# A three-part encoder layer in split fp32: pinning the loads of the SwiGLU tiles and beginning the weight sums one slab earlier

## The chip, the cores and the metric

The kernel runs on one core of one Trainium2 chip. The metric is the device time of one execution in microseconds (us), the median of several runs; lower is better. Beside it there is one execution recorded by the hardware profiler, with a trace of every instruction on every engine. TensorE multiplies, VectorE (DVE) and ScalarE (ACT) work elementwise, GpSimd (POOL) does here little more than issue DMAs, and SyncE (SP) issues the other DMAs.

## The reference

One encoder layer over 256 tokens of width 2048 in float32, ending with a norm. Cut to what matters here:

```
x = x + mix(rms_norm(x)) @ w_out                 # four mixers side by side
x = x + cross_attention(rms_norm(x), mem_n)
h = rms_norm(x)
gate, up = split(h @ w_gate_up)                  # 2048 -> 2 * 5632
x = x + (silu(gate) * up) @ w_down               # 5632 -> 2048
out = rms_norm(x)
```

The change lies in the third part, the SwiGLU.

## The kernel before

**Weights.** All weights lie in one tensor, in the order of use. It is cut into slabs of 128 x 2048 floats (1024 KB), and a slab holds sixteen 128 x 128 blocks. A slab is read into a `raw` buffer by SP (four such buffers during this stage) and each float is split into a high part `wh` (ACT, a cast) and a low part `wl` (DVE, a subtraction), because TensorE multiplies in a shorter format; three products (high by high, high by low, low by high: lines 472 to 474) stand for one fp32 product. The pieces that ACT and DVE produce are called halves here. The kernel makes them five ahead of TensorE (`_fill`, with a ring of five buffers), so that ACT and DVE wait for TensorE when all is well.

**The SwiGLU's first half, `gate_up`.** The 5632 columns are worked in groups of 512, eight slabs to a group: group 0 apart, and then groups j = 1 to 10, each through `paired_rows` after a plan of eight letters:

```
GROUPS = *["NSSNSSNN"] * 9, "NSNSNSNN"
```

A slab marked N is used as it is, by 24 products. A slab marked S holds two rows and two columns of blocks that are worked as in Strassen's method, with 21 products instead of 24; `z` holds the combined forms of the activations, and sums of the weights are needed too. So a group of four N and four S has 4 x 24 + 4 x 21 = 180 products. The S slabs of a group are called S1, S2, S4 and S5 below, by their place in the plan.

**The sums of an S slab.** Two of the sums are not made by DVE but by a DMA that adds. While some earlier slab is loaded (`_load`), SP reads the slab's last 512 columns into a buffer `t` (line 114; one of four tiles named `res`), ACT copies them to the buffer's other half (line 119), and GpSimd issues a DMA that adds 1024 further columns of the slab onto them (line 121, `accum_op=ALU.add`). This last one is called the adding DMA below. The ACT copy stands in a kept place: `keep` (which is `keep_place`) ties an instruction to the one that stands before it on its engine, so that the scheduler of the compiler, which otherwise reorders the instructions of an engine as they come ready, leaves it there. `AHEAD` says how many slabs before its own slab this is begun: two. So the sums of S1, S2, S4 and S5 are begun at the slabs 7 (of the group before), 0, 2 and 3 of a group, and a slab counts as loaded in program order right before its first half is made. ACT splits the summed buffer in the third of the S slab's four steps (line 178, `wh<-res`), and DVE adds with it in the second (line 189, `raw<-res,raw`).

**The way of a SwiGLU tile.** At the end of a group, `up` makes silu(gate) * up, turns it (DVE, line 597) and GpSimd stores it (line 599, two DMAs named `hidden<-g`), four tiles of 128 x 256 in a group and 44 in all. For the second half of the SwiGLU the tiles are read back (`load_turned`, line 604, `tmp<-hidden`) into `tmp` buffers, of which there are eleven, and split into `f` tiles. The first 22 are read and split during `gate_up` by the generator `fetch`, which `begin` calls at the first three N slabs of a group; the other 22 are queued after the loop with a second `fetch`. GpSimd issues its DMAs one after the other, and one that waits for something holds up all that stand behind it in GpSimd's line.

`self.bg.now` is TensorE's time as the kernel counts it while the program is written (0.68 us for three products), and `stored[j]` is its value when group j's storing was written down.

Of the kernel before, what the change touches and what calls it, by code (L numbers as in the profile page):

```python
# [28 lines left out]
FT = DFF // P  # L29
# [19 lines left out]

PAIRED = {a + i for a, plan in [(GATE_UP + 8 * j, GROUPS[j % len(GROUPS)]) for j in range(10)] + [(DOWN, PASSES[0]), (DOWN + 22, PASSES[1])]  # L50
          for i, x in enumerate(plan) if x in "Ss"}
AHEAD = (-2, -2)

SUMS = [{GATE_UP + 8 * j + i + a: GATE_UP + 8 * j + i for j in range(10) for i, x in enumerate(GROUPS[j % len(GROUPS)]) if x == "S"}
        for a in AHEAD]

# [236 lines left out]
class Block:  # L293
# [805 lines left out]
    def gate_up(self, gp, f, z):  # L1099

        nc = self.nc
        box, g, stored = {}, {}, []

        def gate(ps):
            for r in range(2):
                g[r] = gp.tile([P, 512], F32, name=f"g{r}", tag=f"g{r}")
                nc.scalar.activation(g[r], ps[r], AF.Silu, scale=box["col"][:, r:r + 1])

        def up(j, ps, h=None):
            h = h or [gp.tile([P, 512], F32, name="h", tag="h", bufs=2) for _ in range(2)]  # L1110
            for r in range(2):
                self.stt(h[r], ps[r], box["col"][:, r:r + 1], g[r], ALU.mult, ALU.mult)
                self.store_turned(self.ff, 4 * j, r, g[r], h[r])
            stored.append(self.bg.now)

        def mixed(q1, q5, q6, q7):

            g[0], g[1], h[0], h[1] = (gp.tile([P, 512], F32, name=n, tag=n, bufs=b) for n, b in (("g0", 1), ("g1", 1), ("h", 2), ("h", 2)))
            nc.scalar.copy(g[0], q1)
            self.tt(h[0], g[0], q6, ALU.add)  # L1120
            self.tt(g[1], h[0], q7, ALU.add)
            self.tt(h[0], q5, h[0], ALU.subtract)
            self.tt(h[1], q5, g[1], ALU.subtract)

        def gated(*ps):

            for r in range(2):
                self.tt(g[r], g[r], ps[r], ALU.add)
                nc.scalar.activation(g[r], g[r], AF.Silu, scale=box["col"][:, r:r + 1])

        def upped(j, ps):

            for r in range(2):
                self.tt(h[r], h[r], ps[r], ALU.add)
            up(j, h, h)

        h = {}

        def fetch(k0, k1, ahead, pause, wait=0):

            m = {}
            for k in range(k0, k1 + ahead):
                if k < k1:
                    while len(stored) <= k // 4:
                        yield
                    m[k] = self.tmp()
                    self.load_turned(m[k], self.ff, k)
                if k >= k0 + ahead:
                    while k0 == 0 and k - ahead >= 20 and "free" not in box:
                        yield  # L1150
                    while wait and self.bg.now < stored[(k - ahead) // 4] + wait:
                        yield
                    mark = self.mark()
                    self.split(f[k - ahead], m.pop(k - ahead))
                    self.keep_place(mark)
                    self.have = k - ahead + 1
                    yield pause

        def norm():

            mark = self.mark()
            nc.scalar.activation(self.mg[:, 0:1], self.mg[:, 0:1], AF.Silu)
            self.keep_place(mark)
            yield 2.0
            self.row_norm(1, box)
            yield

        arp = ExitStack()
        ar = arp.enter_context(self.tc.tile_pool(name="arp", bufs=4))
        arrival = lambda: ar.tile([P, R], F32, name="ar", tag="ar")  # L1170
        last = self.bg.add(self.arrive(self.xf[1], 3, arrival, self.put3, FAR), go=True)
        col = self.bg.add(norm())

        def combined():
            for ks, z in sums:
                yield 3.0
                yield from self.combine(z, *(self.h3[k] for k in ks))

        sums = [((2 * i, 2 * i + 1), z[(i + 1) % 4]) for i in range(4)]
        comb = self.bg.add(combined())  # L1180
        whole = [self.whole(c) for c in range(4)]

        def before(n):
            if n == 1:
                self.st.lend(self.wz)
                self.st.sums = list(whole)
            if n in (1, 3):
                self.bg.drain(self.late if n == 1 else last)
            if n == 3:
                self.leave(3)  # L1190

        ps = self.gemm_rows("w_gate_up", [0, DFF], self.h3,
                            parts=[(range(8), [0]), (range(8, 12), [0]), (range(12), [1]), (range(12, 16), [0]), (range(12, 16), [1])],
                            before=before)
        self.bg.drain(col)
        arp.close()
        more = ExitStack()
        rx = more.enter_context(self.tc.tile_pool(name="rawx", bufs=1))
        self.st.raws.append([rx, -1])
        gate(ps[0])  # L1200
        up(0, ps[1])
        early = fetch(0, FT - 22, 3, 2.0, 15)
        self.bg.drain(comb)
        for j in range(1, DFF // 512):
            plan = GROUPS[(j - 1) % len(GROUPS)]
            if j == 10:
                box["free"] = True
            turns = [i for i, x in enumerate(plan) if x == "N"][:3]

            def begin(i):  # L1210

                if (j, i) == (10, 5):
                    self.st.back(self.wz, rx)
                if i in turns:
                    next(early, None)

            upped(j, self.paired_rows("w_gate_up", [j * 512, DFF + j * 512], self.h3, sums[:8 - plan.count("N")], plan, mixed, gated,
                                      before=begin, swap=j % 2 == 0)[0])
        more.close()
        for c, x in enumerate(whole):  # L1220
            nc.sync.dma_start(x, self.rd[:, c * 1024:(c + 1) * 1024])
        for _ in early:
            pass
        self.fetch = self.bg.add(fetch(FT - 22, FT, 6, SOON))

    def down(self, f, sp):
# [752 lines left out]
```

## Time and profile before

| | us |
|---|---|
| median of 3 runs (1444.95 to 1450.44) | 1446.47 |
| profiled execution | 1453.54 |
| its span in the trace | 1451.7 |
| TensorE products, busy | 1427.3 |
| VectorE busy | 1176.1 |
| ScalarE busy | 850.3 |
| GpSimd busy | 243.3 |

The profiled execution is 1.84 us longer than its span and 7.07 us longer than the median of the runs. In rows of a timeline the columns are: start, duration, engine, line, operation, what is written from what, how many, and in brackets the engine's idle time before it with what ended that time. `PEclk` in a row of stages is the TensorE clock that was granted, as a share of full speed.

### The profile page before, as it was taken

The page shows a single profiled execution, that of the slowest core. Times are in us where ns is not written, and L with a number is a line of the kernel's source. Part 1 is how long each engine was busy: PE and PEld are TensorE (multiplying, and loading weights), DVE is VectorE, ACT ScalarE, POOL GpSimd, SP SyncE. Part 2 cuts the span into 40 slices and gives each one's busy share as a digit, 9 for nine tenths or more (in the row PEclk, how much of TensorE's full clock was granted, in tenths as well). Part 3 has the DMA queues.
Part 4 walks back from the last instruction along what each step waited for, and adds up shares of the span by engine and source line. Part 5 has one row for each costly group of instructions (what it writes and reads, how often), then busy time and mean ns, then how long its engine had stood idle before and what let it go on. Part 6 is the DMA issues. An engine that isn't in the chain of part 4 may idle for free.

```text
span 1451.7 us, 18644 instructions
## 1 busy us (share of the span) xinstructions
PE 1427.3 (98%) x6562; PEld 1178.6 (81%) x6562; DVE 1176.1 (81%) x1782; ACT 850.3 (59%) x1242; POOL 243.3 (17%) x315
## 2 busy tenths in 40 slices
PE   9999999999999999999999999999999999999997
PEld 7888888888888888888888877778878888788885
DVE  6668868777977676676688988889988988989997
ACT  6556555446655555555565666656656654655655
POOL 0000100012302233530422211222211111100000
PEclk9999999999999999999999999999999999999999
DMA  9887564456657788964998999999999986665554
GB/s 345 293 287 249 201 216 152 168 187 225 200 196 226 243 266 260 271 195 149 292 298 250 273 272 272 262 273 240 272 258 280 275 269 205 200 237 191 187 223 145
DMA packets 72461, 344.84 MB, mean 238 GB/s; under 512 B 10893, under 2 KB 12590, under 8 KB 45744
## 3 DMA queue, kind: packets, MB, share of 16 engines
q1 hardware_dynamic: 52976, 285.31, 57.0%
q0 software_dynamic: 18960, 57.69, 17.3%
q8 instruction: 51, 0.84, 0.2%
q10 hardware_dynamic: 432, 0.66, 0.1%
q14 instruction: 42, 0.34, 0.1%
HBM read 321.07 MB, written 22.54 MB: 237 GB/s over the span
## 4 chain that ended last, share of the span: by engine, by line
PE 75%; issue 13%; DMA 5%; DVE 3%; POOL 2%; ACT 1%; SPq 0%; POOLq 0%; ACTq 0%; DVEq 0%
PE pg L473 18%; PE pg L472 18%; PE pg L474 18%; PE pg L420 4%; PE pm L472 4%; PE pm L473 4%; PE pm L474 4%; PE pg L421 2%; DMA res<-in_W 2%; DMA hidden<-g 1%; DVE wl L179 1%; DMA raw<-in_W 1%; PE pm L1432 1%; POOL tmp L604 1%; POOL res L121 1%
## 5 line engine op out<-in xcount | busy, mean ns | idle before, releaser
L167 DVE TENSOR_TENSOR wl<-raw,wh 128x1024 fp32r<-128x1024 f32 (+1 forms) x395 | 474.5, 1212 | 165.1 <-ACT wh L166 163.2
L166 ACT CAST wh<-raw 128x1024 fp32r<-128x1024 f32 (+1 forms) x395 | 406.2, 1042 | 260.0 <-PE pg L474 193.0
L472 PE MATMUL pg<-wh,act 128*128 128x512 f32 (+1 forms) x1165 | 456.1, 392 | 2.1 <-ACT wh L166 1.9
L473 PE MATMUL pg<-wl,act 128*128 128x512 f32 (+1 forms) x1165 | 454.3, 390 | 1.5 <-DVE wl L167 1.5
L474 PE MATMUL pg<-wh,act 128*128 128x512 f32 (+1 forms) x1165 | 453.9, 390 | 0.0
L472 PEld LDWEIGHTS pg<-wh,act 128*128 128x128 f32 x1165 | 219.1, 188 | 50.6 <-ACT wh L166 3.4
L473 PEld LDWEIGHTS pg<-wl,act 128*128 128x128 f32 x1165 | 219.3, 188 | 47.8 <-DVE wl L167 3.0
L474 PEld LDWEIGHTS pg<-wh,act 128*128 128x128 f32 x1165 | 219.0, 188 | 46.3 <-DVE act L322 0.2
L178 ACT CAST wh<-raw 128x1024 fp32r<-128x1024 f32 (+1 forms) x177 | 161.6, 918 | 144.7 <-DVE raw L189 58.9
L179 DVE TENSOR_TENSOR wl<-raw,wh 128x1024 fp32r<-128x1024 f32 (+1 forms) x177 | 182.9, 1057 | 23.5 <-ACT wh L178 21.8
L473 PE MATMUL pm<-wl,act 128*128 128x512 f32 x290 | 113.0, 390 | 0.2 <-DVE wl L167 0.2
L474 PE MATMUL pm<-wh,act 128*128 128x512 f32 x290 | 112.9, 389 | 0.0
L472 PE MATMUL pm<-wh,act 128*128 128x512 f32 x290 | 112.9, 389 | 0.0
L420 PE MATMUL pg<-act,wh 128*128 128x512 f32 x256 | 90.5, 395 | 0.0
L121 POOL DMA_DIRECT2D res<-in_W x39 | 35.6, 913 | 252.6 <-ACT res L119 244.2
L421 PE MATMUL pg<-act,wl 128*128 128x256 f32 x256 | 71.8, 280 | 0.0
L178 ACT CAST wh<-res 128x1024 fp32r<-128x1024 f32 x39 | 41.1, 1053 | 49.6 <-DMA res<-in_W 33.8
L189 DVE TENSOR_TENSOR raw<-raw 128x512 f32<-128x512 f32 x99 | 68.1, 688 | 1.7
L473 PEld LDWEIGHTS pm<-wl,act 128*128 128x128 f32 x290 | 54.4, 188 | 11.9 <-DVE wl L167 0.5
L472 PEld LDWEIGHTS pm<-wh,act 128*128 128x128 f32 x290 | 54.4, 188 | 11.3
L474 PEld LDWEIGHTS pm<-wh,act 128*128 128x128 f32 x290 | 54.4, 188 | 11.3
L420 PEld LDWEIGHTS pg<-act,wh 128*128 128x128 f32 x256 | 48.1, 188 | 10.5
(376 smaller groups left out, 1937.1 us busy)
## 6 DMA issues: line engine op xcount, KB each, us to landing
raw<-in_W SPq DMA_DIRECT2D x207, 1024.0 KB, 5.3
raw<-in_W SPq DMA_DIRECT2D x39, 768.0 KB, 7.2
res<-in_W POOLq DMA_DIRECT2D x39, 512.0 KB, 9.7
res<-in_W SPq DMA_DIRECT2D x39, 256.0 KB, 5.3
raw<-in_W SPq DMA_DIRECT2D x11, 512.0 KB, 7.4
hidden<-g POOLq DMA_DIRECT2D x22, 256.0 KB, 4.1
tmp<-hidden POOLq DMA_DIRECT2D x44, 128.0 KB, 7.0
features<-tmp POOLq DMA_DIRECT2D x32, 128.0 KB, 4.5
```

The source lines that it names most:

```text
L121: nc.gpsimd.dma_start(t, self.W[SUMS[1][n // 16]][:, 512:1536], accum_op=ALU.add)
L166: nc.scalar.copy(wh[:, a:b], r[:, a:b])
L167: nc.vector.tensor_tensor(out=wl[:, a:b], in0=r[:, a:b], in1=wh[:, a:b].bitcast(F32), op=ALU.subtract)
L178: nc.scalar.copy(wh, src)
L179: nc.vector.tensor_tensor(out=wl, in0=src, in1=wh.bitcast(F32), op=ALU.subtract)
L189: nc.vector.tensor_tensor(out=out, in0=a, in1=b, op=ALU.add)
L420: self.nc.tensor.matmul(p[:, :], wh, slot[:, :], start=start, stop=False)
L421: self.nc.tensor.matmul(p[:, 0:R], wl, slot[:, 0:R], start=False, stop=stop)
L472: self.nc.tensor.matmul(p, hi, wh, start=start, stop=False)
L473: self.nc.tensor.matmul(p, hi, wl, start=False, stop=False)
L474: self.nc.tensor.matmul(p, lo, wh, start=False, stop=stop)
L604: self.nc.gpsimd.dma_start(t.rearrange("p (g t) -> p g t", t=32), src)
```

## The change

Three things are changed.

- `AHEAD` goes from two slabs to three: the sums of S1, S2, S4 and S5 are begun at slabs 6 and 7 of the group before, 1 and 2. All three steps move (SP's read, ACT's copy, GpSimd's adding DMA); none is added.
- The loads of the first 22 tiles are written down only when `bg.now` is 12 us past their group's storing, and each is tied to the GpSimd instruction that stands before it. Before, they were written down as soon as the group was stored, and the scheduler was free to place them; instead the split of a tile waited until 15 us past the storing. Only one of the two waits is left.
- These loads run two tiles ahead of their splits instead of three.

```diff
-AHEAD = (-2, -2)
+AHEAD = (-3, -3)
...
-        def fetch(k0, k1, ahead, pause, wait=0):
+        def fetch(k0, k1, ahead, pause, after=0):
 
             m = {}
             for k in range(k0, k1 + ahead):
                 if k < k1:
                     while len(stored) <= k // 4:
                         yield
+                    while after and self.bg.now < stored[k // 4] + after:
+                        yield
                     m[k] = self.tmp()
+                    mark = self.mark()
                     self.load_turned(m[k], self.ff, k)
+                    if after:
+                        self.keep_place(mark)
                 if k >= k0 + ahead:
                     while k0 == 0 and k - ahead >= 20 and "free" not in box:
-                        yield
-                    while wait and self.bg.now < stored[(k - ahead) // 4] + wait:
                         yield
                     mark = self.mark()
                     self.split(f[k - ahead], m.pop(k - ahead))
...
-        early = fetch(0, FT - 22, 3, 2.0, 15)
+        early = fetch(0, FT - 22, 2, 2.0, 12)
```

The second `fetch`, for tiles 22 to 43, passes no `after`: its loads are neither delayed nor tied. The plan of the groups, four S slabs in nine of them, is as before.

## The prediction

> **What bounds the kernel now.** I read the page first, then TensorE's timeline through `gate_up`, then GpSimd's, then the landing of single DMAs.
>
> ```profile
> span 1451.7 us, 18644 instructions
> PE 1427.3 (98%) x6562; PEld 1178.6 (81%) x6562; DVE 1176.1 (81%) x1782; ACT 850.3 (59%) x1242; POOL 243.3 (17%) x315
> ```
>
> TensorE is busy for all but 24.4 us, so a change can only give back idle time, or time at a lower clock. Where that lies is seen from the first product with a `z` in each of the groups 1 to 10, which is the second step of S1:
>
> ```profile
> 785.26 0.39 PE L472 MATMUL pg<-wh,z 128*128 128x512 f32 x1
> 826.06 0.39 PE L472 MATMUL pm<-wh,z 128*128 128x512 f32 x1
> 868.54 0.39 PE L472 MATMUL pg<-wh,z 128*128 128x512 f32 x1
> 913.84 0.39 PE L472 MATMUL pm<-wh,z 128*128 128x512 f32 x1
> 955.83 0.39 PE L472 MATMUL pg<-wh,z 128*128 128x512 f32 x1
> 1001.50 0.39 PE L472 MATMUL pm<-wh,z 128*128 128x512 f32 x1
> 1042.30 0.39 PE L472 MATMUL pg<-wh,z 128*128 128x512 f32 x1
> 1090.25 0.39 PE L472 MATMUL pm<-wh,z 128*128 128x512 f32 x1
> 1131.54 0.39 PE L472 MATMUL pg<-wh,z 128*128 128x512 f32 x1
> 1172.34 0.39 PE L472 MATMUL pm<-wh,z 128*128 128x512 f32 x1
> ```
>
> The differences are 40.80, 42.48, 45.30, 41.99, 45.67, 40.80, 47.95, 41.29 and 40.80 us. Three groups take 40.80 us, which is a group's 180 products at 0.2267 us; that is the floor. Above it lie 0, 1.68, 4.50, 1.19, 4.87, 0, 7.15, 0.49 and 0: **19.88 us in all** (387.08 less 9 x 40.80).
>
> The cause is one DMA in each group. GpSimd's line in group 3, and then the adding DMA of S5 in the other groups:
>
> ```profile
> 867.36 1.56 POOL L599 DMA_DIRECT2D hidden<-g  x2 [5.18 <-DVE g L597]
> 868.91 0.95 POOL L121 DMA_DIRECT2D res<-in_W  x1
> 873.43 3.57 POOL L604 DMA_DIRECT2D tmp<-hidden  x4 [3.57 <-DMA hidden<-g]
> 876.95 1.00 POOL L121 DMA_DIRECT2D res<-in_W  x1
> 895.90 0.88 POOL L121 DMA_DIRECT2D res<-in_W  x1 [17.96 <-ACT res L119]
> 905.30 0.85 POOL L121 DMA_DIRECT2D res<-in_W  x1 [8.52 <-ACT res L119]
> ...
> 791.69 1.00 POOL L121 DMA_DIRECT2D res<-in_W  x1
> 833.52 1.01 POOL L121 DMA_DIRECT2D res<-in_W  x1
> 920.56 0.99 POOL L121 DMA_DIRECT2D res<-in_W  x1
> 964.23 0.99 POOL L121 DMA_DIRECT2D res<-in_W  x1
> 1007.31 1.00 POOL L121 DMA_DIRECT2D res<-in_W  x1
> 1052.42 0.99 POOL L121 DMA_DIRECT2D res<-in_W  x1
> 1096.75 0.99 POOL L121 DMA_DIRECT2D res<-in_W  x1
> 1137.58 0.88 POOL L121 DMA_DIRECT2D res<-in_W  x1 [5.08 <-ACT res L119]
> ```
>
> In group 3 the storing is issued, then the adding DMA of S4 (868.91). Four tile loads follow, which wait 3.57 us for the storing to land and take 3.57 us to issue, and only then comes the adding DMA of S5 (876.95). Counted from the group's first `z` product, S5's goes out at 6.43, 7.46, 8.41, 6.72, 8.40, 5.81, 10.12, 6.50 and 6.04 us in groups 1 to 9. Set beside the excess: nothing up to 6.43, 0.49 at 6.50, 1.19 at 6.72, 1.68 at 7.46, 4.50 and 4.87 at 8.4, 7.15 at 10.12. The excess follows this one time in order; from 6.50 to 10.12 it grows by 6.66 in 3.62 us, **1.84 us per us late, from a knee at about 6.3**. It also lands later than its neighbours. These are the landing times of the DMAs of 868.91 and 876.95, and ACT's wait for the second:
>
> ```profile
> DMA to landing us min/median/max: 9.9/9.9/9.9
> DMA to landing us min/median/max: 13.1/13.1/13.1
> 890.16 1.05 ACT L178 CAST wh<-res 128x1024 fp32r<-128x1024 f32 x1 [5.10 <-DMA res<-in_W]
> ```
>
> 876.95 and 13.1 is 890.05; ACT starts at 890.16, and TensorE, five halves behind, runs dry. The slope is steeper than 1 because the clock is halved after the longer gaps:
>
> ```profile
> 893.00:895.00 2.00, 2.00 (x5) 1.56 (x6) 2.00 (x2) 2.00 (x4) 0.00 (x0) 0.50 0.51 131
> 1066.75 0.80 PE L472 MATMUL pm<-wh,z 128*128 128x512 f32 x1 [2.70 <-ACT wh L178]
> 1068.24 0.80 PE L473 MATMUL pm<-wl,z 128*128 128x512 f32 x1 [0.70 <-DVE wl L179]
> ```
>
> The last number but two of the first row is the granted clock, 0.50 behind the gaps of group 3; in group 7 a product takes 0.80 us instead of 0.39 behind a wait of 2.70. By the Trainium skill, "TensorE: Matmul & The Clock Gate", Part 1, the clock falls only after at least one idle window of about 3.4 us; here it fell behind waits of 2.70 us and 0.70 us, so the trace disagrees. By that rule the 19.88 us would be gaps alone, and I keep the 19.88, which the group starts give without it.
>
> **The change part by part.** *Three slabs ahead.* Nothing is added: the same reads, copies and adding DMAs are issued one slab earlier (24 products, 5.44 us, or 21, 4.76 us). What matters is the order on GpSimd. S5's sum is now begun with slab 2 instead of slab 3, and the one begun with slab 2 was so far S4's, the row at 868.91, right behind the storing and ahead of the loads. So S5's adding DMA takes that place. It goes out 0.37 us after the first `z` product in group 3 instead of 8.41, and should land after 9.9 us instead of 13.1. In group 2 the place is
>
> ```profile
> 825.53 0.95 POOL L121 DMA_DIRECT2D res<-in_W  x1
> 1043.40 0.96 POOL L121 DMA_DIRECT2D res<-in_W  x1
> ```
>
> at -0.53, and in group 7, the worst, at +1.10. So S5's time falls to between -0.5 and 1.1, at least 5.2 us short of the knee of 6.3, and the excess goes. The cover is five halves of work already made; if S5's were still late by d past the knee, 1.84 d per group comes back.
>
> What is late next? Halves are made five ahead, four to an S slab and two to an N slab, so the moment at which a sum is begun can be counted in TensorE's time: S4's moves from the start of S1 to the start of slab 7 before it (10.9 us earlier, and ahead of the storing), S1's from S5's third step to its first (2.04 us), S2's from the start of slab 6 to S5's third step (2.72 us). S1's and S2's were at 895.90 and 905.30. S1 of group 4 starts at TensorE at 913.16 (its first `z` less 0.68), S2 4.76 us later at 917.92. The leads were 17.3 and 12.6 us and become 19.3 and 15.3. S1's and S2's now go out 2 us apart; if the second queues behind the first, it may land as S5's does now, after 13.1. S5's knee stands for a lead of 12.7 (S5 starts 19.04 us after the first `z` product, and 19.04 - 6.3 is 12.7), so 15.3 holds with 2.6 to spare. No adding DMA is late next. Each buffer `t` is last read eight slabs before its next S slab, and ACT's copy now comes five slabs later, some 25 us, so SP's read between the two has room. Price: nothing, with 0 to 2 us a group if S2's margin fails by about 1.
>
> *The loads in a kept place.* Same number; 22 of 44 are tied. They go one at a time, in the turns at slabs 0, 3 and 6, behind the GpSimd instruction written before: the storing, S5's or S2's adding DMA. At slab 0 no load of the newest group is old enough, and at slab 3 the count is 14.96 us, which passes 12 (it did not pass 15). One load costs 0.9 us of GpSimd (3.57 / 4). The one behind the storing stands ahead of S5's DMA: 1.10 + 0.9 = 2.0, still 4.3 short of the knee. The one behind S5's may wait for the storing to land, and nothing stands behind it for two slabs. Nothing to pay.
>
> *Two ahead, 12 us.* In the steady state a tile is loaded two turns, at least 20 us, before its split. Only in group 1 are tiles 0 to 2 written down in one turn together with the split of tile 0. They cannot go before the storing has landed, which was at 791.69 - 3.57 = 788.1, and the turn at slab 3 comes at 785.26 - 5.44 - 0.68 + 14.96 = 794.1. The landing of the tile loads in this stage:
>
> ```profile
> DMA to landing us min/median/max: 3.0/7.5/9.6
> ```
>
> 788.1 + 9.6 = 797.7, so ACT may stand for up to 3.6 us, once, against five halves of cover. I take 0.5, with 0 to 3.6.
>
> Sum for the profiled execution: 1453.54 - 19.88 + 0.5 = 1434.2. The median of the runs was 7.07 below that execution, and the trace does not show in which stage. If none of it belongs to these stalls, the median becomes 1446.47 - 19.4 = 1427.1; if all of it does, 1446.47 - 12.3 = 1434.2. I take the middle: **1431**, 1426 to 1436.
>
> **The rivals.** *The DMA engines become the bound.* Rows for the worst stretch, and for two groups at the floor:
>
> ```profile
> 832.00:1136.00 304.00, 293.18 (x1255) 238.74 (x1254) 271.72 (x326) 188.25 (x234) 58.36 (x67) 0.98 0.93 265
> 785.00:826.00 41.00, 41.00 (x182) 33.96 (x181) 38.07 (x46) 27.31 (x34) 8.26 (x10) 1.00 0.96 276
> 1001.00:1042.00 41.00, 41.00 (x182) 33.95 (x182) 37.46 (x45) 27.55 (x35) 6.95 (x9) 1.00 0.97 277
> ```
>
> The last two numbers are the DMA engines' share and GB/s. 304 us at 265 GB/s hold 80.6 MB for (304 - 19.88) / 40.80 = 6.96 groups, 11.57 MB each; at the floor that is 284 GB/s. If 277 is the ceiling a group takes 41.8 us, 1.0 over the floor; seven groups keep 7 of the 19.88 us. The gain is then 5.5 to 12.5 by the same two readings of the median, about 1437.5. For it: shares of 0.97. Against: ACT's waits name the adding DMA and never a `raw` buffer's in this stage. VectorE has 271.72 / 6.96 = 39.0 us of work in a group of 40.80, close, but it held the floor in both rows.
>
> By the Trainium skill, "DMA: Bandwidth & Descriptors", Anatomy of one DMA, a GpSimd DMA takes about 2.0 us and its bytes over 436 GB/s: 3.2 us for these 512 KB as an estimate. The rows have 9.9 and 13.1. By it S5's would land in time already and the change could give nothing, which is what the next rival gives.
>
> *The change does not do what it says.* If the scheduler again put loads ahead of S5's, or its copy waited as long as before, all stays: 1446.5. Against: in the rows above the loads stand behind what was begun with slab 2, in groups 2, 3 and 7 alike.
>
> *Slower.* A tied load that waits for a free `tmp` now holds S5's DMA, which may not pass it, in groups 7 to 9, where the untied loads fill the eleven buffers.
>
> ```profile
> 1219.00 0.90 POOL L604 DMA_DIRECT2D tmp<-hidden  x1 [6.52 <-DVE z L322]
> ```
>
> This one waited 6.52 us. If it waits a whole turn (14.96), S5's goes out at 2 + 15 = 17, 10.7 past the knee: 19.7 us a group. Two such groups give back 39.4 against 19.9: +19.5, or 1466. It decides once the waits past the knee sum to 10.8 us. Against: few tied loads are under way at a time, and they are older than the untied ones.
>
> **How the numbers follow.** Stalls go 0.72 (1431), DMA bound 0.13 (1437.5), no effect 0.06 (1446.5), slower 0.09 (1466). A measurement can tell about 0.5%, 7.2 us. Faster: 0.72 and most of 0.13, 0.82; same 0.09; slower 0.09. The range 1425 to 1440 leaves out the last two and the tails.
>
> **What would show it.** First `z` products 40.8 us apart; S5's adding DMA right behind the storing, landing in about 10; no half clock in `gate_up`; clumps of loads only behind the storing of groups 5 to 7. Wrong if the groups stay at 42 or more with S5's early (another bound), or if GpSimd waits for buffers ahead of an adding DMA.

## The result

| | before | after |
|---|---|---|
| median of the runs, us | 1446.78 | 1435.07 |
| lowest to highest | 1444.95 to 1450.44 | 1434.24 to 1435.35 |
| profiled execution | 1453.54 | 1435.07 |
| its span | 1451.7 | 1433.3 |

The change makes the kernel faster by 0.85%: the ratio is 0.9915, with a 95% interval of 0.9895 to 0.9935. Measured again beside other kernels the changed one had 1435.22 (1434.19 to 1436.29) against 1451.86 (1443.91 to 1457.18) before, a ratio of 0.9890 (0.9858 to 0.9922). The changed kernel repeats its time; the kernel before spreads over some 15 us in all its runs, so the size of the gain depends on which of its executions are met.

The first product with a `z` in each group, in the trace of the changed kernel (timeline of TensorE; the first, then groups 8, 9 and 10):

```profile
784.67 0.39 PE L472 MATMUL pg<-wh,z 128*128 128x512 f32 x1
...
1070.27 0.39 PE L472 MATMUL pm<-wh,z 128*128 128x512 f32 x1
...
1111.07 0.39 PE L472 MATMUL pg<-wh,z 128*128 128x512 f32 x1
...
1154.52 0.39 PE L472 MATMUL pm<-wh,z 128*128 128x512 f32 x1
```

Groups 1 to 8 take 40.80 us each (1111.07 - 784.67 is 8 x 40.80), the floor. Only group 9 takes 43.45, 2.65 more. Of the 19.88 us lost before, 17.23 are back, and the span is 18.4 us shorter. GpSimd's line in group 4 (first `z` product at 907.07), and in group 8 (1070.27):

```profile
905.13 1.58 POOL L599 DMA_DIRECT2D hidden<-g  x2 [9.42 <-DVE g L597]
906.68 0.92 POOL L604 DMA_DIRECT2D tmp<-hidden  x1
907.57 0.99 POOL L121 DMA_DIRECT2D res<-in_W  x1
908.16 1.31 POOL L604 DMA_DIRECT2D tmp<-hidden  x1
927.80 0.88 POOL L121 DMA_DIRECT2D res<-in_W  x1 [18.33 <-ACT res L119]
930.23 0.87 POOL L121 DMA_DIRECT2D res<-in_W  x1 [1.54 <-ACT res L119]
...
1068.32 1.57 POOL L599 DMA_DIRECT2D hidden<-g  x2 [9.41 <-DVE g L597]
1069.88 0.90 POOL L604 DMA_DIRECT2D tmp<-hidden  x1
1070.77 0.97 POOL L121 DMA_DIRECT2D res<-in_W  x1
1071.36 6.57 POOL L604 DMA_DIRECT2D tmp<-hidden  x7
1081.77 0.89 POOL L604 DMA_DIRECT2D tmp<-hidden  x1 [3.84 <-DMA res<-in_W]
1083.06 0.88 POOL L604 DMA_DIRECT2D tmp<-hidden  x1 [0.41 <-issue]
```

In group 4 S5's adding DMA goes out at 907.57, 0.50 us after the `z` product, with one load ahead of it and one behind. In group 8 it does the same, but then nine loads follow: seven at once and two more. They are the first of the untied second 22 tiles (tile 21 is the load at 1069.88). The eighth came later because it waited for S5's DMA to land (1070.77 + 10.7 is 1081.47). What the clump does is seen in the DMAs of 1070 to 1090 us (size and time to landing), and in ACT's waits of 1070 to 1122:

```profile
raw<-in_W SPq DMA_DIRECT2D x3, 1024.0 KB, 14.2
tmp<-hidden POOLq DMA_DIRECT2D x10, 128.0 KB, 11.9
...
ACT wh L166 <- DMA raw<-in_W: 3.9, 2, 2.3
...
ACT wh L178 <- DMA raw<-in_W: 1.8, 1, 1.8
```

Whole weight slabs land after 14.2 us beside the clump, and ACT waits three times for a slab to land in `raw`, 5.7 us in all; from 785 to 1070 such waits came to 0.9 us. The halves fall behind, and TensorE runs dry in the first S slab of group 9:

```profile
1114.58 0.50 PE L473 MATMUL pm<-wl,z 128*128 128x512 f32 x1 [1.77 <-DVE wl L179]
```

The rows of two stretches, one within groups 2 to 7 and one of group 9:

```profile
832.00:1070.00 238.00, 238.00 (x1051) 197.08 (x1051) 227.28 (x276) 158.95 (x200) 44.56 (x52) 1.00 0.94 282
1111.00:1154.00 43.00, 40.96 (x180) 33.25 (x179) 40.67 (x49) 26.72 (x33) 4.66 (x6) 1.00 0.86 269
```

In the first, TensorE has no idle microsecond in 238, at full clock, with the DMA engines moving 282 GB/s at a share of 0.94.

### The profile page after: what moved, and what is told of

The parts are those of the page before. It is cut to its first block, busy times and chain, and to the rows that moved or that the text cites. A ratio compares the mean times of both kernels' runs of the same rounds, so it can differ in the third digit from the quotient of the medians.

```text
span 1433.3 us, 18659 instructions
## 1 busy us (share of the span) xinstructions
PE 1418.9 (99%) x6562; PEld 1175.2 (82%) x6562; DVE 1174.3 (82%) x1782; ACT 850.3 (59%) x1242; POOL 243.3 (17%) x315
## 4 chain that ended last, share of the span: by engine, by line
PE 94%; DVE 3%; DMA 2%; ACT 1%; issue 0%; SPq 0%; ACTq 0%; DVEq 0%
PE pg L473 21%; PE pg L474 21%; PE pg L472 21%; PE pm L472 7%; PE pm L473 7%; PE pm L474 6%; PE pg L420 4%; PE pg L421 2%; DMA raw<-in_W 2%; PE pm L1435 1%; DVE wl L179 1%; PE pm L1073 1%; PE pm L1044 1%; DVE wl L167 1%; DVE raw L189 0%; ACT wh L178 0%
## 5 line engine op out<-in xcount | busy, mean ns | idle before, releaser
L604 POOL DMA_DIRECT2D tmp<-hidden x44 | 43.9, 1058 | 37.6 <-DVE z L322 13.7
```

Source lines behind the costliest of these rows:

```text
L604: self.nc.gpsimd.dma_start(t.rearrange("p (g t) -> p g t", t=32), src)
```

## The experiments

Three theories were tried against each other. "Place": the loss came from S5's adding DMA standing behind the loads in GpSimd's line. "Lead": the sums needed one more slab, wherever the loads stood. "Clump": four loads at once slowed all that landed beside them.

**Three slabs ahead alone.** The kernel before with

```diff
-AHEAD = (-2, -2)
+AHEAD = (-3, -3)
```

> The sums begun three slabs ahead, with the tile loads as before: free to be placed, four in a clump behind the storing. Theory 'place': the loss was S5's adding DMA standing behind the four loads, and one slab more puts it ahead of them. Then the clumps stay, S5's goes out -0.5 to 1.5 us after the group's first z product, groups take 40.8 us and the median is 1433 to 1437. Rival 'lead' (S5's needed a slab more, wherever the loads stand): the same. Rival 'clump' (four loads at once on the DMA engines slow all that lands beside them, and spreading them was the cure): groups of 42 to 44 us remain and the median is 1443 to 1448.

1432.77 us (1431.80 to 1433.45), ratio 0.9898 (0.9877 to 0.9920). All nine groups took 40.80 us: the trace lost nothing. GpSimd's line in group 3, the first `z` product at 867.34:

```profile
865.39 1.56 POOL L599 DMA_DIRECT2D hidden<-g  x2 [9.43 <-DVE g L597]
866.95 0.95 POOL L121 DMA_DIRECT2D res<-in_W  x1
869.95 3.57 POOL L604 DMA_DIRECT2D tmp<-hidden  x4 [2.05 <-DMA hidden<-g]
```

The clump of four is there as before, but S5's DMA (866.95) is ahead of it and landed after 10.1 us. So "clump" falls for clumps of four that come behind S5's, and half of the change brings all of the gain.

**Tied loads alone.** The changed kernel with `AHEAD = (-2, -2)`.

> The tile loads tied and spread as in the changed kernel, with the sums begun two slabs ahead as before. 'Place': S5's adding DMA no longer has four loads in front of it and goes out when slab 2 starts at TensorE, 10.2 - 6.1 = 4.1 us after the first z product, under the knee of 6.3; groups take 40.8 to 41.5 us, median 1435 to 1439. 'Lead': two slabs are too few, 1443 to 1448. 'Clump': 1434 to 1437.

1443.55 us (1439.23 to 1445.39), ratio 0.9963 (0.9945 to 0.9981). The median is where "lead" put it, but the trace says otherwise. Groups 2 to 7 took 40.80 us each, with S5's DMA at 5.78 us after the `z` product; group 1 took 46.69 and group 8 47.47. In group 8 nine loads clump again. S5's went out at 5.78 us there too (1081.02), but five of them had been issued just ahead of it. Its landing, and ACT's wait for it:

```profile
DMA to landing us min/median/max: 17.1/17.1/17.1
...
1098.22 1.04 ACT L178 CAST wh<-res 128x1024 fp32r<-128x1024 f32 x1 [6.46 <-DMA res<-in_W]
```

So here S5's was issued in time and landed late, which is what "clump" says. In the kernel before, too, S5's behind four loads took longer to land (13.1 us in group 3) than S4's ahead of them (9.9). In group 1 it is the first tile (GpSimd's line, then ACT's):

```profile
789.54 0.87 POOL L121 DMA_DIRECT2D res<-in_W  x1 [5.12 <-ACT res L119]
790.11 3.01 POOL L604 DMA_DIRECT2D tmp<-hidden  x3
...
802.40 0.40 ACT L330 CAST act<-tmp 128x256 fp32r<-128x256 f32 x1 [7.92 <-DMA tmp<-hidden]
```

Tiles 0 to 2 are tied behind S5's DMA, which now comes later, and the split of tile 0 is written in the same turn in a kept place. ACT stood 7.92 us for it. The 12.56 us of this kernel's trace are costs that came with the tying, not the old loss. The same ties cost 2.65 us with three slabs ahead, so in the changed kernel the third slab covers most of them.

**The loads ahead of S5's again, at three slabs.** The changed kernel, with (in `begin`, and in `_load`; `fetch` then splits these tiles without loading them again)

```diff
+                if i == 0:
+                    for k in range(4 * j - 4, min(4 * j, FT - 22)):
+                        clump[k] = self.tmp()
+                        mark = self.mark()
+                        self.load_turned(clump[k], self.ff, k)
+                        self.keep_place(mark)
...
+            mark = len(nc.cur_bb.bb.instructions)
             nc.gpsimd.dma_start(t, self.W[SUMS[1][n // 16]][:, 512:1536], accum_op=ALU.add)
+            self.keep(mark)
```

> The changed kernel with three slabs ahead, but in groups 1 to 6 the loads of the four (in group 6 two) tiles just stored are tied right behind the storing, and the adding DMAs are tied too, so that S5's stands behind the loads again. 'Place': S5's goes out 6.5 to 8.5 us after the first z product and lands after 12 to 13; by the slope of 1.84 us per us past 6.3 the trace loses 2 to 20 us over groups 1 to 6, and the median is 1437 to 1446. 'Lead': three slabs are enough, 1433 to 1437 and groups of 40.8 us. 'Clump': 1441 to 1446, S5's landing late wherever it stands.

1437.43 us (1435.86 to 1438.30), ratio 0.9930 (0.9908 to 0.9952): at the low edge of "place". Line 604 is 606 here and 121 is 122. Group 4, first `z` product at 910.49:

```profile
909.20 1.57 POOL L601 DMA_DIRECT2D hidden<-g  x2 [9.97 <-DVE g L599]
916.27 3.52 POOL L606 DMA_DIRECT2D tmp<-hidden  x4 [5.50 <-issue]
919.78 0.96 POOL L122 DMA_DIRECT2D res<-in_W  x1
...
930.72 1.05 ACT L180 CAST wh<-res 128x1024 fp32r<-128x1024 f32 x1 [3.71 <-DMA res<-in_W]
```

S5's went out at 8.31, 6.55, 7.02, 9.29, 7.41 and 5.71 us in groups 1 to 6, and the excess was 3.80, 0, 0, 1.70, 0.38 and 0.08. So the loss comes back with the place though the sums are begun three slabs ahead, 5.96 us against none in the first experiment. But it comes back smaller than in the kernel before, where 9.15 and 9.27 cost over 5 us (below), and not in the order of these times.

The landing puts it in order. Here S5's landed 20.3, 18.0, 18.0, 20.1, 18.8 and 13.6 us after the first `z` product, because from issue to landing it took 7.9 to 12.0 us. In all 27 groups of the three traces of the kernel before, S5's landed by 18.4 in each group that lost nothing and after 18.7 in each group that lost something: 0.27 us for 18.7, 1.19 for 19.65, 1.68 and 1.75 for 20.1 and 20.2, 4.50 for 21.5, 7.15 for 23.2. Group 4 here has 1.70 for 20.1, and group 8 of the tied loads alone 6.67 for 22.9. So it is the landing that must not be late. The place in GpSimd's line is one part of that, and the time to landing is the other. Group 1 here lost more than its 20.3 accounts for because the clock stood at one half for 3.4 us from 808.2 on, which costs 1.7.

**The clump of nine.** The changed kernel again, three slabs alone again, and the changed kernel with the first of the second 22 loads tied as well, one in each turn from group 8 on (the second `fetch` then finds them in `second` and does not load them again):

```diff
                 if i in turns:
                     next(early, None)
+                    if (j, i) > (8, 0):
+                        k = FT - 22 + len(second)
+                        second[k] = self.tmp()
+                        mark = self.mark()
+                        self.load_turned(second[k], self.ff, k)
+                        self.keep_place(mark)
```

> The changed kernel once more, beside the next three. The loss of its group 9 (2.65 us in the trace, behind a clump of nine loads in group 8) should be there again; median 1434 to 1436.

> Three slabs ahead alone, once more, beside the changed kernel. If tying the loads costs by the clump of nine alone, it is 2 to 3 us faster than the changed kernel: 1432 to 1433.5, all groups at 40.8 us. If the first 2.3 us were a difference of chips or calls, the two are equal within 0.7 us.

> The changed kernel, and the first loads of the second 22 tiles also tied, one in each turn from group 8 on, so that there is no clump of nine. 'Clump' (nine loads at once held up the weight reads of group 8): all groups at 40.8 us, 1432 to 1433.5. Rival: group 9's loss comes from the adding DMA of S4 (32.07 us after the first z product instead of 28.58), whatever the clump: it stays, 1434.5 to 1436.

On one chip: the changed kernel 1435.22 (1434.19 to 1436.29), three slabs alone 1432.25 (1431.52 to 1433.18), the spread version 1431.77 (1431.54 to 1433.32). In the traces group 9 lost 3.96, 0 and 0 us. The weight reads of the same stretch of group 8 in the spread version:

```profile
raw<-in_W SPq DMA_DIRECT2D x3, 1024.0 KB, 8.6
```

8.6 us instead of 14.2. The rival was S4's adding DMA, which goes out at 32.07 us in group 8 of the changed kernel and at 28.58 here. It is not what starved TensorE: both of its waits in group 9 (1.77 us at 1114.58 and 0.28 at 1119.92) come before S4 begins, at 1128.0. So the clump of nine costs the changed kernel some 3 us, and nothing else in the tying costs anything.

**Two slabs, with the loads in good places.** The last kernel with `AHEAD = (-2, -2)`, and the first split one turn later:

```diff
+                if after and k == k0 + ahead:
+                    yield pause
```

> As the last one, but the sums begun two slabs ahead, and the split of the first tile one turn after its load. 'Place': with no loads in front of S5's and no clump, two slabs are enough; S5's goes out at 5.8 us, all groups at 40.8 us, 1432 to 1435. 'Lead': the third slab is needed at least in some groups, 1437 to 1445.

1432.16 us (1431.57 to 1432.88), all nine groups at 40.80 us, S5's DMA at 5.78 to 5.82. S5's landed 15.7 to 16.9 us after the first `z` product. The third slab is not needed when nothing stands in front of S5's. "Lead" falls, "place" holds. These three versions (three slabs alone, spread, two slabs spread) beat both kernels, and cannot be told from each other.

**The kernel before, twice more.**

> The kernel before, a second trace. If its loss is the adding DMA of S5 behind the loads, the excess of a group follows that DMA's time again (nothing up to about 6.4 us after the first z product, some 1.8 us per us past it), and the sum over groups 1 to 9, though another number than 19.88, explains the execution's time: span = 1431 + the sum, within 2 us. Rival: the spread of its executions lies in other stages; then the sum stays near 20 and the span differs.

> A third trace of the kernel before, for the same two readings.

Executions of 1451.51 and 1447.05 us, spans 1449.7 and 1445.3; the groups lost 19.92 and 15.37 us, and 1431 plus these is 1450.9 and 1446.4. Between these two the whole difference lies in this stage. The first trace was some 2 us longer outside it as well (1451.7 less 19.88 is 1431.8, against 1429.8 and 1429.9). Over the 27 groups of its three traces the excess and S5's time agree (correlation 0.96; a line through those later than 6.5 us has a slope of 1.95 and meets zero at 6.33), with single groups off by 1 to 2: 7.38 cost 3.92, and 7.85 cost 1.75. Those two landed at 20.8 and 20.2, and only the first has the clock at one half, for 3.4 us. At 9.15 and 9.27 it was 5.32 and 5.80.

## Why the prediction was right, and where it missed

The direction and the mechanism held, and 1435.07 lies in the range of 1425 to 1440. The gain was 11.7 us where 15.5 were forecast (1446.47 less 1431); in the second measurement, against slower executions of the kernel before, it was 16.6.

*What bounds the kernel.* Right: excess and S5's time belong together, and the later traces gave the knee and nearly the slope again. The knee is one in the landing, though, at about 18.5 us, and the prediction counted it in the time of issue. In the kernel before the two go together; in the experiments they did not.

*Three slabs ahead.* Right: S5's adding DMA took S4's place and went out between -0.39 and 0.82 us in groups 2 to 8, where -0.5 to 1.1, or 2.0 with a load ahead, was foreseen; it landed after 9.6 to 10.7 us. S1's and S2's go out 2.4 us apart, and the second lands after 10.9 to 12.4, inside the 15.3 worked out for it. That lead was miscounted, on the safe side: S2's sum went out 9.26 us earlier (23.16 us after the first `z` product, against 32.42 in the two-slab spread version) and not 2.72, so its lead is 21.7. The 2 us apart of the prediction does not go together with its own 19.3 and 15.3 either, since S2 starts 4.76 us after S1.

*The loads in a kept place: "nothing to pay".* This is the step that failed. The clumps were expected behind the storing of groups 5, 6 and 7, a few loads each. No untied load came before the last tied one (tile 21, at 1069.88), and then nine came together. That fits `tmp` buffers given out in program order: eleven, less those of tiles 20 and 21. In the kernel before, the same nine had gone out in three clumps, from 1005.56 on; there the load of tile 21 stands at 1004.68. The term was 0 and measured 2.65 us in one trace and 3.96 in the other, 3.0 to 3.5 in the medians. With it the forecast would have been about 1434.

*The first tile.* Taken at 0.5 with 0 to 3.6; ACT waited 0.80 us in the changed kernel, and TensorE lost nothing:

```profile
793.80 0.41 ACT L330 CAST act<-tmp 128x256 fp32r<-128x256 f32 x1 [0.80 <-DMA tmp<-hidden]
```

The bound was too narrow for such a wait: the tied loads alone, at two slabs, showed 7.92.

*The step to the median.* The middle was taken between two readings, for want of a trace that could decide. The loss of the kernel before is another in each execution (19.88, 19.92 and 15.37 in three), while the changed kernel's profiled execution equals its median. Of the 6.49 us between the profiled execution (1453.54) and the third trace's (1447.05), 4.51 lie in this stage. So most of the 7.07 us belonged to the stalls, and some of it did not. The middle was a fair guess: the three versions that lose nothing in the stage have medians of 1431.8 to 1432.8. The changed kernel lies above it by its clump. The profiled execution lay in the upper part of what the kernel before showed in all its runs, 1442 to 1457 us.

*The rivals.* The DMA engines were no bound: 282 GB/s at a share of 0.94 with TensorE never idle, above the 277 taken as a ceiling. A tied load that waits for a buffer ahead of S5's was not seen: the long wait of a load in group 8 (3.84 us at 1081.77) is one of an untied load, stands behind S5's, and ended as S5's landed. The change gave what the landing times in the rows had led to; by the Trainium skill, "DMA: Bandwidth & Descriptors", Anatomy of one DMA, these 512 KB would land in an estimated 3.2 us, and no adding DMA of the two traces, before and after, did so in less than 5.7. What the parts are worth is now known: the three slabs alone bring all of the gain. The tying also takes the old loss out of groups 2 to 7, but alone, as it stands, it puts 12.56 us in its place; spread further and with the first split later, it brings all of the gain too. With the three slabs there is nothing left for it to bring, and its clump costs some 3 us.

## What to carry to other kernels

When a late transfer starves the kernel, look at when it lands, and then at what stands before it in its issuer's line. Here the cure was its place, and an earlier start or a moved neighbour gave the same. An instruction that is tied in its place pushes what is left untied somewhere else, so look for where that lands. A kernel whose executions spread, with a trace of one of them, should have its gain read against the spread and not against that trace alone.

## What the runs showed of the hardware

The granted clock fell to one half behind waits of TensorE shorter than I had expected. In the changed kernel's second trace a single wait of 2.04 us was enough (the stretch behind it), and in the first trace a wait of 1.77 us was not:

```profile
1116.00:1118.00 2.00, 2.00 (x6) 1.52 (x6) 1.97 (x4) 0.00 (x0) 0.00 (x0) 0.50 1.05 175
...
1116.00:1118.00 2.00, 2.00 (x11) 1.64 (x10) 2.00 (x3) 0.00 (x0) 0.00 (x0) 1.00 0.92 210
```

Products in 2 us: 6 against 11. The half clock lasted 3.4 us, which costs 1.7. This is why 2.43 us from one product's start to the next, 2.20 more than the usual 0.23, became 3.96 us of loss. But the length of one wait does not decide: with the loads ahead at three slabs, waits of 0.28 and 1.34 us in group 1, 1.8 us apart, were enough (the clock of 808.2 to 811.6 was 0.50). By the Trainium skill, "TensorE: Matmul & The Clock Gate", Part 1, it takes an idle window of about 3.4 us; the runs show less than that.
